# Queueing the modulation's weight blocks earlier in the first part of a hybrid diffusion layer

## The chip, the cores and the metric

One core of a Trainium2 chip runs the whole layer as one program. The metric is device time in microseconds (us) of one execution. TensorE is called PE in the profile, VectorE DVE, ScalarE ACT, GpSimd POOL and SyncE SP; PEld is TensorE's weight load.

## The reference, cut to what matters

The layer takes 512 tokens of width 1024. The change lies in the part before the big input projection, which computes this:

```
x   = x + sincos_2d(512)                              # positions are added
m   = silu(c) @ ada_w + ada_b                         # modulation, 6 x 1024 outputs; the same for c_ctx
h   = sin(fr1 * (z @ w1 + b1)); h = sin(fr2 * (h @ w2 + b2)); h = (h @ w3) * decay    # filter network
kf  = rfft(two-sided kernel made of h)                # spectra of the filters
hx  = rms_norm(x, norm1_g) * (1 + sc1) + sh1          # uses the first 2 x 1024 outputs of m
p   = hx @ w_in                                       # the input projection, everything later needs it
```

Behind it come the context states, the two token mixers (HGRN2 scans and a Hyena long convolution through the spectra `kf`), the merge, the output projection and a mixture of 32 experts (top group, top two experts), whose weights are 190 MB.

## The kernel before, in words

The kernel is one long function. On PE and DVE the instructions run in the order in which they are written (a manual schedule is entered ahead of the filter network). On ACT, POOL and SP a scheduler chooses the order from its own estimates, and each engine then works through its list in that order.

The first part up to the input projection does these things:

- **Loads.** SP issues them: the decay tables `dec` (4 of 256 KB), the tables of the discrete Fourier transform `tabf` (4 of 256 KB), the tokens `x` (4 of 512 KB, list `xts`), the column positions `cpos` (256 KB), and the weight blocks of the modulation `aw` (8 blocks of 1 MB; the first three are one load each into tiles of the pool `w8`, the others two loads of 512 KB each), then `wi`, the first block of `w_in` (two halves of 512 KB, in pieces of 512 B, name `firsts`). (KB and MB are counted in powers of two.) There are eight load semaphores used in turn: a load is issued only once the load eight places before it has landed, so that the start of one load tells when another one was in.
- **The filter network** (`sin_layer`, twice): a small matmul on PE, six operations on DVE, a sine on ACT. Between the two layers' matmuls and the third one, `warm(W3)` puts six matmuls on zeros on PE.
- **The filters** (`filters(0)`, `filters(1)`): matmuls of the third layer into PSUM tiles `ps_t` (four buffers), multiplied by `dec` on DVE into `hp` and `hm`.
- **The positions** (`placed(i)`): for each of four token tiles a one-pass matmul with the row positions `rowp`, added to the left half of `x` on DVE; POOL adds `cpos` to the right half.
- **The modulation** (`ada_row(k)`, k from 0 to 7): for weight block k four matmuls of the 1024 outputs times two columns (`ccs`, the SiLU of c and c_ctx) into the one PSUM tile `pada`. Each is two passes on PE, so that a row is eight entries in the trace.
- **The spectra of the filters** (`dft_steps`, two generators `ks[0]`, `ks[1]`): each takes four pairs of matmuls, and for every two of them one copy on ACT (`dto`) and two operations on DVE (`spec`).
- **The norm** (`normed(i)`): per token tile on ACT a square with a sum (`junk`), a logarithm (`xs`) and an exponential (`xr`), then on DVE the scaled tokens `xn`.
- **Turning and modulating** (`turned`, `ready`, `rest`): the `xn` are transposed on PE; `pada` is copied (`mr`), transposed and made into the scales `gc` and shifts `sc`; `hraw` and the two parts of `hT` follow. `high` and `low` make the two parts `wh` (ACT) and `wl` (POOL for the first, DVE for the second half) of `wi`. With `hT`, `wh` and `wl` the projection starts, three matmuls for each block.

Before the change, the positions of all four tiles stand behind `filters(1)`, then row 0, half of `ks[0]`, row 1, `normed(0)` and `normed(1)`, the rest of `ks[0]`, row 2, `normed(2)` and `normed(3)`, the transpose of the small parameters `prow`, row 3, half of `ks[1]`, rows 4 and 5, twelve transposes of `xn`, rows 6 and 7, and so on.

The lines of the profile: L136 is `mm` (every matmul), L118 `act` (every ACT operation), L332 the filters' product, L337 and L338 the positions, L343 `xn`, L365 to L369 `spec`, L405 the transpose of `prow`, L419 the transposes of `xn`, L429 `mr`, L440 to L442 `sc` and `gc`, L468 `hraw`, L473 the second part of `hT`; L238, L241, L245, L248, L253, L259, L226 and L227 issue the loads of `dec`, `tabf`, `x`, `cpos`, `aw` (first three), `aw` (halves) and the two halves of `wi`; L1622 and L1624 issue the experts' weights.

Of the kernel before, what the change touches and what calls it, by code (L numbers as in the profile page):

```python
# [18 lines left out]
P = 128  # L19
T = 512  # L20
NT = 4
TC = 256
D = 1024
KD = 8
# [8 lines left out]
N8 = 10  # L33
FIX = 4
W1 = 8
W3 = 6
R2 = 3
ORD = (7, 0, 3, 2, 4, 5, 1, 6)
LEAD = 4
# [29 lines left out]
def kernel(ctx: ExitStack, tc: tile.TileContext, a, out, dbg=None):  # L69
    nc = tc.nc  # L70
# [21 lines left out]
    def ps_t(shape=(P, 512)):  # L92
        return pp.tile(list(shape), F32, name="ps_t", tag="t", bufs=4)

    def th(name, shape=(P, 512), dt=F32):

        return fp.tile(list(shape), dt, name=name, tag="h", bufs=NB)
# [9 lines left out]
    def ta(name, shape=(P, 2, 512), dt=F32):  # L107

        return mid.tile(list(shape), dt, name=name, tag="a", bufs=NA)

    def unit(name, shape, dt=F32):

        return base.tile(list(shape), dt, name=name, tag="w8", bufs=NU)
# [11 lines left out]
    def act_set(name):  # L125

        p = nc.scalar.preload_act_table_set(name)
        for r in users:
            tc.add_manual_dep(p.ins, r.ins.name, NOSYNC, reason="activation table")
        users.clear()  # L130
        gate[0] = p
# [3 lines left out]
    def mm(o, l, r, start=True, stop=True):  # L135
        nc.tensor.matmul(o, l, r, start=start, stop=stop)  # L136
# [59 lines left out]
    def warm(n):  # L196

        p = ps_t()
        for i in range(n):
            mm(p, zero[:, 0:P], zero)  # L200
# [22 lines left out]
    def columns2(c0, c1):  # L223

        w = unit("wi", (P, 2, KD, P))
        nc.sync.dma_start(w[:, 0], w_in_v[:, :, c0:c0 + P])  # L226
        nc.sync.dma_start(w[:, 1], w_in_v[:, :, c1:c1 + P])  # L227
        return w[:, 0], w[:, 1]
# [4 lines left out]
        nc.sync.dma_start(w, w_in_v[:, :, c0:c0 + 256])  # L233
        return w[:, :, 0:P], w[:, :, P:2 * P]

    dec = [th(f"dec{m}") for m in range(4)]
    for m in (0, 2, 1, 3):
        nc.sync.dma_start(dec[m], a["k_dec"][m])  # L238
    tabf = [th(f"tabf{m}", (P, 2, 256)) for m in range(4)]
    for m in range(4):  # L240
        nc.sync.dma_start(tabf[m], a["k_tabf"][:, m])  # L241
    xts = []
    for i in range(NT):
        x = ta("x", (P, D))
        nc.sync.dma_start(x, a["x"][0, i * P:(i + 1) * P, :])  # L245
        xts.append(x)
    cpos = th("cpos")
    nc.sync.dma_start(cpos, a["k_cpos"])  # L248
    aws = []
    for k in range(KD):  # L250
        if k < NU:
            w = unit("aw", (P, 2048))
            nc.sync.dma_start(w, ada_v[:, k, 0:2048])  # L253
            aws.append([w[:, j * 512:(j + 1) * 512] for j in range(4)])
        else:
            aws.append([])
            for j in range(2):
                w = ta("aw")
                nc.sync.dma_start(w.rearrange("p a b -> p (a b)"), ada_v[:, k, j * D:(j + 1) * D])  # L259
                aws[k] += [w[:, 0], w[:, 1]]  # L260
        if k == KD - 2:
            firsts = columns2(2560, 3072)

# [2 lines left out]
    def ada_row(k):  # L266
        for j in range(4):
            mm(pada[32 * j:32 * j + 32], ccs[:, k, :], aws[k][j], k == 0, k == KD - 1)
# [19 lines left out]
    def sin_layer(ps, b, f, nm):  # L288
        x = tj(nm + "a", (P, 256))
        V.tensor_scalar(x, ps, pf[:, b:b + 1], pf[:, f:f + 1], op0=OP.add, op1=OP.mult)  # L290
        n = tj(nm + "n", (P, 256))
        V.tensor_scalar(n, x, 1.0 / (2.0 * math.pi), MAGIC, op0=OP.mult, op1=OP.add)
        V.tensor_scalar(n, n, MAGIC, None, op0=OP.subtract)
        V.scalar_tensor_tensor(x, n, -TWO_PI_HI, x, op0=OP.mult, op1=OP.add)
        V.scalar_tensor_tensor(x, n, -TWO_PI_LO, x, op0=OP.mult, op1=OP.add)
        V.tensor_scalar(x, x, 3.1415925, -3.1415925, op0=OP.min, op1=OP.max)
        s = tj(nm + "s", (P, 256))
        act(s, x, AF.Sin)
        return s
# [4 lines left out]
        r = slice(64 * h, 64 * h + 64)  # L304
        mm(pz[r], fw[r, 1], h1[r])
    h2f = sin_layer(pz, 2, 3, "f2")
    warm(W3)
    act_set(EXPLN)


# [10 lines left out]
    def filters(m):  # L321

        ph = []
        for j in range(2):
            for h in range(2):
                r = slice(64 * h, 64 * h + 64)
                ph.append(ps_t())
                mm(ph[-1], h2f[r, m * P:(m + 1) * P], w3[j][r])
        for h in range(2):
            for j, (dst, nm) in enumerate(((hp, "hp"), (hm, "hm"))):  # L330
                dst[m + 2 * h] = tj(f"{nm}{m + 2 * h}")
                V.tensor_mul(dst[m + 2 * h], ph[2 * j + h], dec[m + 2 * h])  # L332

    def placed(i):
        x, p = xts[i], ps_t()
        mm(p, rowp[:, 1, i * P:(i + 1) * P], rowp[:, 0])
        V.tensor_add(x[:, 0:512], x[:, 0:512], p)  # L337
        G.tensor_add(x[:, 512:1024], x[:, 512:1024], cpos)  # L338

    def normed(i):  # L340
        r = rstd_of(xts[i], "x", th("junk", (P, D), BF))
        xn.append(ta("xn", (P, D)))
        V.tensor_scalar(xn[i], xts[i], r, None, op0=OP.mult)  # L343

    def dft_steps(b, srcs_c, srcs_s, new, r, hold=False, tabs=None):

        for cs, src in ((0, srcs_c), (2, srcs_s)):
            p2 = []
            for par in range(2):
                p = ps_mm() if hold and cs and not par else ps_t()  # L350
                for aa in range(2):
                    bs = slice(b * P, (b + 1) * P)
                    if tabs is None:
                        mm(p, tabf[cs + par][:, aa, bs], src[par * 2 + aa], aa == 0, aa == 1)
                    else:
                        mm3(p, tuple(x[:, aa, bs] for x in tabs[cs + par]), src[par * 2 + aa], aa == 0, aa == 1)
                p2.append(p)
                if par == 0:
                    yield
            if hold and cs:  # L360
                yield
            o = th("dto")
            act(o, p2[1], AF.Copy)
            x, y = new()
            V.tensor_add(x, p2[0], o)  # L365
            if cs == 0:
                V.tensor_sub(y, p2[0], o)
            else:
                V.tensor_sub(y, o, p2[0])  # L369
            r += [x, y]  # L370
            yield
# [12 lines left out]
    x, y = hp[0][0:1], hm[0][0:1]  # L384
# [1 line left out]
    V.tensor_scalar(y, x, 0.5, None, op0=OP.mult)  # L386
    V.tensor_scalar(x, x, 0.5, None, op0=OP.mult)
    filters(1)
    for i in range(NT):
        placed(i)  # L390
    ada_row(0)
    kf = [[], []]
    ks = [dft_steps(b, hp, hm, new_a, kf[b], b == 1) for b in range(2)]
    next(ks[0])
    next(ks[0])
    ada_row(1)
    normed(0)
    normed(1)
    next(ks[0])
    next(ks[0])  # L400
    ada_row(2)
    normed(2)
    normed(3)
    pt = ps_t((P, P))
    nc.tensor.transpose(pt, prow, ident)  # L405
    V.tensor_copy(prm, pt)
    ada_row(3)
    next(ks[1])
    next(ks[1])
    ada_row(4)  # L410
    ada_row(5)

    hT = []
# [739 lines left out]
    for n in range(8):  # L1153
        x, e = tj("gb"), tj("gs")
# [111 lines left out]
    for i in range(NT):  # L1266
        x = ta("xacc", (P, D))
# [183 lines left out]
    f = [finish(i) for i in range(NT)]  # L1451
# [680 lines left out]
```

## Time and profile before

| | |
|---|---|
| three runs | 1037.67, 1035.18, 1037.04 us, median 1037.04 |
| profiled execution | 1041.55 us, its span 1039.7 us |
| PE busy | 964.7 us, 93% of the span |
| DVE, ACT, POOL busy | 528.3, 298.3, 184.5 us |
| first 60 us | PE busy 48.43 us, DMA share 0.97, 335 GB/s |
| mean granted clock of PE | 0.961 |

The busy time of an engine is a sum over stages with different limits, and a busy PE is not at its peak, since the ends of matmuls are modelled. The chain of work that ended last says which engine had to be waited for at each moment. A row of the timeline gives start, duration, engine, line, operation, tiles, count, and in brackets how long the engine was idle before it and what ended that.

### The profile page before, as it was taken

The numbers are of one execution on the slowest core, as the hardware profiler recorded it, in microseconds if no ns is written. First come the engines' busy times: TensorE is split into PE (matmuls) and PEld (weight loads), VectorE is DVE, ScalarE is ACT, GpSimd is POOL, SyncE is SP. The second block draws the span as 40 slices with busy tenths as digits, with TensorE's granted clock in tenths as the row PEclk, the third lists the DMA queues.
The fourth block names the chain that finished last, engine by engine and source line by source line (L and its number), as shares of the span: only waits on it lengthen the run. The fifth ranks groups of instructions, "written<-read, shape, count | busy, mean of one in ns | idle before, by whom it ended". The sixth has DMA issues, their size and how long they took to land.

```text
span 1039.7 us, 14041 instructions
## 1 busy us (share of the span) xinstructions
PE 964.7 (93%) x5352; PEld 609.7 (59%) x5352; DVE 528.3 (51%) x886; ACT 298.3 (29%) x492; POOL 184.5 (18%) x212
## 2 busy tenths in 40 slices
PE   6999999999999999999989998999998899978656
PEld 1378888888888887787774463433642245422122
DVE  5565797776775888765375322333232134213024
ACT  1464355475474422243271110000100001000003
POOL 5025244542623310214030000000000000000001
PEclk9999999999999999998999998999998899999877
DMA  9952321121123699346647989999999999999981
GB/s 325 378 157 81 102 61 41 42 82 42 41 77 129 221 278 327 111 155 248 266 184 305 423 346 397 422 421 420 421 381 423 421 420 421 420 420 422 417 297 81
DMA packets 95976, 276.20 MB, mean 266 GB/s; under 512 B 12409, under 2 KB 49365, under 8 KB 72227
## 3 DMA queue, kind: packets, MB, share of 16 engines
q1 hardware_dynamic: 94986, 274.06, 68.6%
q0 software_dynamic: 592, 1.18, 0.4%
q8 instruction: 43, 0.70, 0.3%
q14 instruction: 27, 0.21, 0.1%
q10 hardware_dynamic: 328, 0.04, 0.0%
HBM read 271.05 MB, written 4.21 MB: 265 GB/s over the span
## 4 chain that ended last, share of the span: by engine, by line
issue 45%; PE 41%; DVE 8%; DMA 2%; ACT 2%; POOL 1%; POOLq 0%; SPq 0%; DVEq 0%; ACTq 0%
PE ps_mm L136 31%; PE ps_t L136 8%; DVE wl L147 1%; DMA ew<-in_moe_w_up_dram 1%; DVE yr L632 1%; DMA ada<-in_ada_w_dram 1%; DVE acc L1089 0%; DMA pfr<-in_hy_filt_freq_dram 0%; ACT o L118 0%; DMA cst<-in_k_cst_dram 0%; POOL xacc L2000 0%; PE ps_t L1295 0%; DVE rs L1384 0%; DVE x L517 0%; PE ps_t L929 0%
## 5 line engine op out<-in xcount | busy, mean ns | idle before, releaser
L136 PE MATMUL ps_mm<-hT,wh 128*128 128x512 f32 x768 | 237.6, 391 | 1.3 <-DVE hT L473 0.7
L136 PE MATMUL ps_mm<-ew,xg 128*32 128x512 f32 (+2 forms) x992 | 205.4, 646 | 21.3 <-DMA ew<-in_moe_w_up_dram 15.2
L136 PEld LDWEIGHTS ps_mm<-hT,wh 128*128 128x128 f32 x768 | 144.1, 188 | 31.4 <-DVE hT L473 1.2
L136 PE MATMUL ps_mm<-hT,wl 128*128 128x512 f32 x384 | 155.6, 405 | 1.6 <-DVE wl L147 1.5
L136 PEld LDWEIGHTS ps_mm<-ew,xg 128*32 128x32 f32 (+2 forms) x992 | 63.5, 133 | 149.2 <-issue 106.5
L136 PE MATMUL ps_mm<-ew,hT 128*32 128x512 f32 (+2 forms) x512 | 110.0, 671 | 10.9 <-DMA ew<-in_moe_w_down_dram 10.9
L1713 DVE TENSOR_TENSOR hd<-hd,ps_mm 128x512 f32<-128x512 f32 x13 | 8.9, 688 | 184.2 <-PE ps_mm L136 176.2
L2000 POOL TENSOR_TENSOR xacc<-xacc,fs 128x512 f32<-128x512 f32 x4 | 5.0, 1276 | 481.3 <-ACT o L118 481.3
L136 PEld LDWEIGHTS ps_mm<-hT,wl 128*128 128x128 f32 x384 | 72.2, 188 | 17.0 <-DVE wl L147 2.7
L136 PEld LDWEIGHTS ps_mm<-ew,hT 128*32 128x32 f32 (+2 forms) x512 | 31.7, 137 | 83.2 <-issue 62.8
L147 DVE TENSOR_TENSOR wl<-wi,wh 128x1024 fp32r<-128x1024 f32 x46 | 59.5, 1296 | 23.4 <-ACT wh L118 23.1
L118 ACT ACTIVATE wh<-wi 128x1024 fp32r<-128x1024 f32 x48 | 50.7, 1057 | 48.7 <-PE ps_mm L136 40.1
L1749 DVE TENSOR_TENSOR xacc<-xacc,ps_t 128x512 f32<-128x512 f32 x96 | 58.9, 681 | 0.0
L1726 DVE SCALAR_TENSOR_TENSOR ps_mm<-ps_mm,si,gt 128x512 f32<-128x512 f32 x24 | 18.2, 759 | 78.7 <-PE ps_mm L136 77.4
L118 ACT ACTIVATE yh<-ps_mm 128x512 fp32r<-128x512 f32 x24 | 14.3, 598 | 133.6 <-DVE ps_mm L1726 133.6
L1089 DVE SCALAR_TENSOR_TENSOR acc<-ada,ccs,acc 128x512 f32<-128x512 f32 x56 | 43.0, 832 | 0.0
L136 PE MATMUL ps_t<-yl,ohw 128*128 128x512 f32 x100 | 42.5, 425 | 0.0
L118 ACT ACTIVATE hT<-ps_t 128x512 f32<-128x512 f32 x13 | 7.8, 600 | 118.6 <-PE ps_t L1719 109.2
L136 PE MATMUL ps_mm<-woh,mix 128*128 128x512 f32 x112 | 40.6, 419 | 0.0
L136 PE MATMUL ps_t<-yh,ohw 128*128 128x512 f32 x100 | 39.7, 397 | 0.0
L136 PE MATMUL ps_t<-oh,h2l 128*128 128x512 f32 (+1 forms) x96 | 37.9, 395 | 0.0
L136 PE MATMUL ps_t<-oh,h2h 128*128 128x512 f32 (+1 forms) x96 | 36.1, 376 | 0.0
(450 smaller groups left out, 1550.9 us busy)
## 6 DMA issues: line engine op xcount, KB each, us to landing
ew<-in_moe_w_gate_dram SPq DMA_DIRECT2D x64, 1024.0 KB
ew<-in_moe_w_up_dram SPq DMA_DIRECT2D x62, 1024.0 KB
ew<-in_moe_w_down_dram SPq DMA_DIRECT2D x56, 1024.0 KB
ada<-in_ada_w_dram SPq DMA_DIRECT2D x64, 256.0 KB
wi<-in_w_in_dram SPq DMA_DIRECT2D x24, 512.0 KB
wi<-in_w_in_dram SPq DMA_DIRECT2D x12, 1024.0 KB
ew<-in_moe_w_down_dram SPq DMA_DIRECT2D x16, 512.0 KB
aw<-in_ada_w_dram SPq DMA_DIRECT2D x10, 512.0 KB
```

Of the source, the lines that this page charges most:

```text
L118: r = nc.scalar.activation(o, i, f, **kw)
L136: nc.tensor.matmul(o, l, r, start=start, stop=stop)
L147: V.tensor_sub(lo, view, hi)
L632: V.tensor_sub(yr, yr, t)
L1089: V.scalar_tensor_tensor(acc, w, ccs[:, k, 0:1], acc, op0=OP.mult, op1=OP.add)
L1713: V.tensor_mul(hd, hd, gu[1])
L1726: V.scalar_tensor_tensor(p, p, si[:, 1:2], g, op0=OP.mult, op1=OP.mult)
L1749: V.tensor_add(xs, xs, p)
L2000: G.tensor_mul(xs, xs, fs)
```

## The change

Three moves in the first part:

1. The weight blocks' loads are put in a function `ada_block(k)`. Blocks 0 and 1 are queued first of all, block 2 behind `dec`, block 3 behind `tabf`; the tokens and `cpos` come behind those, then blocks 4 to 7 with `wi` as before.
2. `ada_row(0)` and `ada_row(1)` take the place of the six matmuls on zeros behind the second sine layer.
3. `placed` moves from behind `filters(1)` to behind half of `ks[0]` and row 3; the norms and the spectra behind it are written in another sequence.

```diff
@@ -33,7 +33,6 @@
 N8 = 10
 FIX = 4
 W1 = 8
-W3 = 6
 R2 = 3
 ORD = (7, 0, 3, 2, 4, 5, 1, 6)
 LEAD = 4
@@ -233,21 +232,9 @@
         nc.sync.dma_start(w, w_in_v[:, :, c0:c0 + 256])
         return w[:, :, 0:P], w[:, :, P:2 * P]
 
-    dec = [th(f"dec{m}") for m in range(4)]
-    for m in (0, 2, 1, 3):
-        nc.sync.dma_start(dec[m], a["k_dec"][m])
-    tabf = [th(f"tabf{m}", (P, 2, 256)) for m in range(4)]
-    for m in range(4):
-        nc.sync.dma_start(tabf[m], a["k_tabf"][:, m])
-    xts = []
-    for i in range(NT):
-        x = ta("x", (P, D))
-        nc.sync.dma_start(x, a["x"][0, i * P:(i + 1) * P, :])
-        xts.append(x)
-    cpos = th("cpos")
-    nc.sync.dma_start(cpos, a["k_cpos"])
     aws = []
-    for k in range(KD):
+
+    def ada_block(k):
         if k < NU:
             w = unit("aw", (P, 2048))
             nc.sync.dma_start(w, ada_v[:, k, 0:2048])
@@ -258,6 +245,26 @@
                 w = ta("aw")
                 nc.sync.dma_start(w.rearrange("p a b -> p (a b)"), ada_v[:, k, j * D:(j + 1) * D])
                 aws[k] += [w[:, 0], w[:, 1]]
+
+    dec = [th(f"dec{m}") for m in range(4)]
+    tabf = [th(f"tabf{m}", (P, 2, 256)) for m in range(4)]
+    ada_block(0)
+    ada_block(1)
+    for m in (0, 2, 1, 3):
+        nc.sync.dma_start(dec[m], a["k_dec"][m])
+    ada_block(2)
+    for m in range(4):
+        nc.sync.dma_start(tabf[m], a["k_tabf"][:, m])
+    ada_block(3)
+    xts = []
+    for i in range(NT):
+        x = ta("x", (P, D))
+        nc.sync.dma_start(x, a["x"][0, i * P:(i + 1) * P, :])
+        xts.append(x)
+    cpos = th("cpos")
+    nc.sync.dma_start(cpos, a["k_cpos"])
+    for k in range(4, KD):
+        ada_block(k)
         if k == KD - 2:
             firsts = columns2(2560, 3072)
 
@@ -304,7 +311,8 @@
         r = slice(64 * h, 64 * h + 64)
         mm(pz[r], fw[r, 1], h1[r])
     h2f = sin_layer(pz, 2, 3, "f2")
-    warm(W3)
+    ada_row(0)
+    ada_row(1)
     act_set(EXPLN)
 
 
@@ -386,28 +394,26 @@
     V.tensor_scalar(y, x, 0.5, None, op0=OP.mult)
     V.tensor_scalar(x, x, 0.5, None, op0=OP.mult)
     filters(1)
-    for i in range(NT):
-        placed(i)
-    ada_row(0)
+    ada_row(2)
     kf = [[], []]
     ks = [dft_steps(b, hp, hm, new_a, kf[b], b == 1) for b in range(2)]
     next(ks[0])
     next(ks[0])
-    ada_row(1)
+    ada_row(3)
+    for i in range(NT):
+        placed(i)
+    next(ks[0])
+    next(ks[0])
     normed(0)
     normed(1)
-    next(ks[0])
-    next(ks[0])
-    ada_row(2)
+    ada_row(4)
+    next(ks[1])
+    next(ks[1])
     normed(2)
     normed(3)
     pt = ps_t((P, P))
     nc.tensor.transpose(pt, prow, ident)
     V.tensor_copy(prm, pt)
-    ada_row(3)
-    next(ks[1])
-    next(ks[1])
-    ada_row(4)
     ada_row(5)
 
     hT = []
```

How the instructions stand on three engines, before and after. In these lists a number behind a name tells tiles of one name apart, and a semaphore in brackets is what the instruction waits for (DMAHW are the load semaphores).

The load queue, SP, in the stretch from the last tokens to the first block of `w_in`. Before:

```order
L245 DMA x<-in_x_dram 128x1024
L248 DMA cpos<-in_k_cpos_dram 128x512
L253 DMA aw<-in_ada_w_dram 128x2048 x3
L259 DMA aw<-in_ada_w_dram 128x1024 x8
L226 DMA wi<-in_w_in_dram 128x8x128
L227 DMA wi<-in_w_in_dram 128x8x128
L259 DMA aw<-in_ada_w_dram 128x1024 x2
```

Now:

```order
L246 DMA aw<-in_ada_w_dram 128x1024 x2
L262 DMA x<-in_x_dram 128x1024 x4
L265 DMA cpos<-in_k_cpos_dram 128x512
L246 DMA aw<-in_ada_w_dram 128x1024 x6
L225 DMA wi<-in_w_in_dram 128x8x128
L226 DMA wi<-in_w_in_dram 128x8x128
L246 DMA aw<-in_ada_w_dram 128x1024 x2
```

Before, three of the four token loads stood ahead of `dec`; now four blocks of `aw`, `dec` and `tabf` are ahead of all tokens. The loads ahead of `wi` are the same ones in another sequence.

ACT, from the second copy of `ks[0]` to the one of `ks[1]` (`wh_424` and `wh_426` are the two halves' first parts, `dto_315` the second copy of `ks[0]`, `junk` to `xr` one norm). Before:

```order
L118 ACTIVATE dto_315<-ps_t_312 128x512 [waits PE_49]
L118 ACTIVATE junk_324,xs_325<-x_133 128x1024 [waits DMAHW5_49,DVE_49,Pool_49]
L118 ACTIVATE xs_325<-xs_325,eps_t_88 128x1 [waits Activation_49]
L118 ACTIVATE xr_328<-xs_325 128x1 [waits Activation_49]
L118 ACTIVATE junk_332,xs_333<-x_135 128x1024 [waits DMAHW6_49,DVE_49,Pool_49]
L118 ACTIVATE xs_333<-xs_333,eps_t_88 128x1 [waits Activation_49]
L118 ACTIVATE xr_336<-xs_333 128x1 [waits Activation_49]
L118 ACTIVATE wh_424<-wi_161 128x1024 [waits DMAHW3_49]
L118 ACTIVATE wh_426<-wi_161 128x1024 [waits DMAHW4_49]
L118 ACTIVATE dto_353<-ps_t_350 128x512 [waits PE_49]
```

Now, from the first copy of `ks[0]` (`dto_269`) on, with `dto_300` its second copy:

```order
L117 ACTIVATE dto_269<-ps_t_266 128x512 [waits PE_49]
L117 ACTIVATE wh_417<-wi_161 128x1024 [waits DMAHW3_49]
L117 ACTIVATE wh_419<-wi_161 128x1024 [waits DMAHW4_49]
L117 ACTIVATE dto_300<-ps_t_297 128x512 [waits PE_49]
L117 ACTIVATE junk_305,xs_306<-x_139 128x1024 [waits DMAHW0_49,DVE_49,Pool_49]
L117 ACTIVATE xs_306<-xs_306,eps_t_88 128x1 [waits Activation_49]
L117 ACTIVATE xr_309<-xs_306 128x1 [waits Activation_49]
L117 ACTIVATE junk_313,xs_314<-x_141 128x1024 [waits DMAHW1_49,DVE_49,Pool_49]
L117 ACTIVATE xs_314<-xs_314,eps_t_88 128x1 [waits Activation_49]
L117 ACTIVATE xr_317<-xs_314 128x1 [waits Activation_49]
L117 ACTIVATE dto_331<-ps_t_328 128x512 [waits PE_49]
```

The two conversions of `wi` stood behind all four norms; now they stand ahead of all four norms and of the second copy of `ks[0]`.

PE, around the transpose of `prow` (the one with `cst,prow`; `aw,ccs` is a modulation row, `hp` and `hm` with `tabf` the spectra). Before:

```order
L136 MATMUL ps_mm<-aw,ccs 32x512 x4
L405 MATMUL ps_t<-cst,prow 128x128
L136 MATMUL ps_mm<-aw,ccs 32x512 x4
L136 MATMUL ps_t<-hp_231,tabf_121 128x512
L136 MATMUL ps_t<-hp_250,tabf_121 128x512
L136 MATMUL ps_t<-hp_235,tabf_122 128x512
L136 MATMUL ps_t<-hp_254,tabf_122 128x512
L136 MATMUL ps_mm<-aw,ccs 32x512 x8
L419 MATMUL ps_mm<-cst,xn 128x128 x12
L136 MATMUL ps_mm<-aw,ccs 32x512 x8
```

Now:

```order
L135 MATMUL ps_mm<-aw,ccs 32x512 x4
L135 MATMUL ps_t<-hp_232,tabf_117 128x512
L135 MATMUL ps_t<-hp_251,tabf_117 128x512
L135 MATMUL ps_t<-hp_236,tabf_118 128x512
L135 MATMUL ps_t<-hp_255,tabf_118 128x512
L415 MATMUL ps_t<-cst,prow 128x128
L135 MATMUL ps_mm<-aw,ccs 32x512 x4
L425 MATMUL ps_mm<-cst,xn 128x128 x12
L135 MATMUL ps_mm<-aw,ccs 32x512 x8
```

Between the first half of `ks[1]` and the twelve transposes of `xn` there were two rows; now there are the transpose of `prow` and one row. Rows 6 and 7 stand behind the twelve transposes in both.

## Rows read from the trace of the kernel before

**Rows 1.** Busy time by stage: stretch, length, PE, PEld, DVE, ACT, POOL, clock, DMA, GB/s.
```profile
60.00:480.00 420.00, 417.37 (x2563) 351.47 (x2561) 309.83 (x450) 194.69 (x309) 149.97 (x174) 1.00 0.39 127
```
**Rows 2.** SP's waits from 560 to 620 us: waiter, releaser, total us, times, longest.
```profile
SPq L1624 <- PE ps_mm L136: 30.5, 7, 14.9
SPq L1622 <- PE ps_mm L136: 13.7, 2, 11.1
```
**Rows 3.** The chain that ended last, up to 52 us: start, length, what.
```profile
24.20 0.58 PE ps_t L136
...
26.57 1.86 PE ps_mm L136 x8
...
32.68 1.00 PE ps_mm L136 x8
33.68 3.63 PE ps_t L136 x8
...
45.04 1.46 PE ps_mm L419 x12
46.51 1.85 PE ps_mm L136 x16
...
50.67 0.81 DVE hraw L468
```
**Rows 4.** Timeline of DVE: the last scaled token tile.
```profile
41.23 0.75 DVE L343 TENSOR_SCALAR xn<-x,xr 128x1024 f32<-128x1024 f32 x1 [0.85 <-ACT xr L118]
```
**Rows 5.** Timeline of PE between the sine layers and the filters, 12 to 17 us.
```profile
13.09 2.74 PE L136 MATMUL ps_t<-zero 128*128 128x512 bf16 x6
16.27 0.70 PE L136 MATMUL ps_t<-w3s,f2s 64*128 64x512 f32 x2 [0.44 <-ACT f2s L118]
```
**Rows 6.** PE by short stretches: length, busy (count), granted clock, DMA share, GB/s.
```profile
21.00:22.00 1.00, 0.32 (x1) 1.00 0.96 401
...
23.00:24.00 1.00, 0.00 (x0) 0.50 1.00 418
...
29.50:30.00 0.50, 0.50 (x3) 0.86 1.00 401
...
38.00:39.00 1.00, 1.00 (x13) 1.00 1.09 284
```
**Rows 7.** Timeline of SP's load issues (start, length, line, load).
```profile
10.79 0.33 SPq L241 DMA_DIRECT2D tabf<-in_k_tabf_dram  x1
...
13.43 0.33 SPq L248 DMA_DIRECT2D cpos<-in_k_cpos_dram  x1
...
20.16 0.33 SPq L259 DMA_DIRECT2D aw<-in_ada_w_dram  x1
22.64 0.33 SPq L259 DMA_DIRECT2D aw<-in_ada_w_dram  x1
...
30.20 3.97 SPq L227 DMA_DIRECT2D wi<-in_w_in_dram  x1
```
**Rows 8.** Timeline of POOL: the column positions, four tiles.
```profile
20.28 5.61 POOL L338 TENSOR_TENSOR x<-x,cpos 128x512 f32<-128x512 f32 x4 [10.48 <-DMA cpos<-in_k_cpos_dram]
```
**Rows 9.** Timeline of ACT, 32 to 45 us.
```profile
32.72 0.60 ACT L118 ACTIVATE dto<-ps_t 128x512 f32<-128x512 f32 x1 [15.29 <-PE ps_t L136]
33.21 1.05 ACT L118 ACTIVATE junk<-x 128x1024 bf16<-128x1024 f32 x1
...
34.82 1.04 ACT L118 ACTIVATE junk<-x 128x1024 bf16<-128x1024 f32 x1
...
39.45 1.04 ACT L118 ACTIVATE junk<-x 128x1024 bf16<-128x1024 f32 x1
...
41.05 1.04 ACT L118 ACTIVATE wh<-wi 128x1024 fp32r<-128x1024 f32 x1
42.67 1.06 ACT L118 ACTIVATE wh<-wi 128x1024 fp32r<-128x1024 f32 x1 [0.58 <-DMA wi<-in_w_in_dram]
43.63 0.58 ACT L118 ACTIVATE dto<-ps_t 128x512 f32<-128x512 f32 x1
```

## The prediction

> **What bounds the kernel now.** I first read busy time by stage, to see whether a shift in the first part reaches the end. From 60 to 480 us PE is busy 417.37 of 420 us [rows 1]: the reader is to see that there is no gap in which lost time could be made up. Later the load queue is what runs full, but at the start of the expert stage it is PE that holds it back: between 560 and 620 us SP waits 30.5 + 13.7 us for PE to free weight buffers [rows 2]. So a shift of the first part moves the start of that stream with it, and is worth its full size at the end.
>
> Then the chain of waits for the first part [rows 3]. From 24 to 50 us it runs through PE: spectra, modulation rows, from 45.04 twelve transposes of the scaled tokens (1.46 us), rows 6 and 7 from 46.51 (1.85 us), which end at 46.51 + 1.85 = 48.36; behind them the scales are made and `hraw` starts at 50.67, and from there the projection follows. The norms are not on it: the last `xn` ends at 41.23 + 0.75 = 41.98 [rows 4], 3.1 us before its transposes.
>
> **The change part by part.**
>
> *Rows 0 and 1 for the six matmuls on zeros.* The zeros took 2.74 us from 13.09, and PE then waited for the second sine, until 16.27 [rows 5]. A row takes 1.00 us at full clock and 1.86 us in the stretch where the granted clock was 0.50 [rows 3, 6]. Two rows are 2.0 to 3.7 us from 13.2, so they end between 15.2 and 16.9: a delay of the filters of 0 to 0.7 us. The weights are there: block 0 is the first MB of the queue and block 1 the second. Before, the first MB (two token tiles) was in when the third `tabf` load was issued, 10.79, and the second MB (three token tiles and two of `dec`) when `cpos` was issued, 13.43 [rows 7]. A cost of 0 to 0.7 us, and hidden, as shown below.
>
> *Rows 2 and 3 ahead of the positions.* The modulation still needs rows 6 and 7 behind the transposes, so moving rows earlier shortens only what is ahead of the transposes: there PE no longer has two or three rows of 1.00 us to do. That is a possible gain of up to 3 us, if nothing else holds the transposes.
>
> *Tokens and cpos later.* Ahead of and with `cpos` there are now 8.25 MB in the queue (blocks 0 to 3 are 4, `dec` 1, `tabf` 1, tokens 2, `cpos` 0.25). Before, it was the load with which 4.25 MB were in, by 20.16; a load of 1 MB then took 22.64 - 20.16 = 2.48 us. The 8.25 MB were in at 30.20, when the second half of `wi` could be issued (the load eight places before it had landed) [rows 7]. The queue was full all along (DMA share 0.96 to 1.00 at 21 to 24 us [rows 6]), so `cpos` lands at about 30.2 now, 10 us later. POOL then needs 5.61 us for the four tiles [rows 8]: last token tile ready at 35.8. With ACT free, one norm more (a copy's distance aside, the rhythm is 34.82 - 33.21 = 1.61 us a tile [rows 9], 2.5 us from `junk` to the end of `xn`) gives a last `xn` at 38.3, earlier than 41.98. By this part alone the change would not be slower.
>
> *The order on ACT.* This is the term that decides. The two conversions of `wi` now stand between the first and the second copy of `ks[0]`, ahead of all four norms. They need `wi`, and `wi` has not become earlier: the same 11.25 MB stand ahead of it, and its second half is issued when 8.25 MB are in, 30.20 as before. Before, the second conversion found its half at 42.67, having waited 0.58 us for it [rows 9]. So ACT now stands still from the end of the first copy (about 29 us) until 41 to 42.67, with all norms behind it; where the conversions came after the norms they waited 0.58 us.
>
> From 42.67 on, by the distances of [rows 9]: the second conversion to the next instruction 0.96 us (42.67 to 43.63); two copies `dto` at 0.49 each (32.72 to 33.21); three norms at 1.61, 4.83; the last one from its `junk` to the end of its `xn`, 39.45 to 41.98, 2.53 us [rows 4, 9]. Sum 0.96 + 0.98 + 4.83 + 2.53 = 9.30, so the last `xn` ends at 51.97, 10.0 us later than before.
>
> On PE the transpose of `prow` waits for the second copy of `ks[0]` (ACT frees its buffer), so from about 40 to 44 us nothing runs there; then come `prow`, row 5 and the first three transposes as their `xn` arrive. The fourth one needs the last `xn`. Nine transposes are left: 9 x 1.46 / 12 = 1.10 us, then rows 6 and 7, 1.85 us [rows 3]. At full clock these end at 51.97 + 2.95 = 54.92, against 48.36: **+6.6 us**.
>
> *The clock.* PE had its last matmul at about 21.3 before (0.32 us of work in the slice from 21 to 22); in the slice from 23 to 24 the granted clock was 0.50, the lower of its two levels, and it was full again between 29.5 and 30, some 5.4 us after PE resumed at 24.20 [rows 3, 6]. Now PE has little to do from 40 to 52 us. At the lower level the two rows cost 2 x (1.86 - 1.00) = 1.7 us more and nine transposes up to 1.1 us more: 0 to 2.8 us. I take 2.6, near the upper end, since the gap is longer than the one in the rows, and the 5.4 us to recovery nearly cover the stretch.
>
> **Sum:** 6.6 + 2.6 = **+9.2 us**. The scales, `hraw` and `hT` follow rows 6 and 7 as before. The earlier terms (filters up to 0.7 us late; the second half of `ks[0]`, 3.63 us, at most twice that at the lower clock) are hidden: their results are wanted by ACT only at 43.63, and before, PE had finished both halves of `ks[0]` at 33.68 + 3.63 = 37.3 [rows 3], 6 us earlier. If that cover were gone they would cost 0.7 to 4.3 us. The profiled execution would be 1041.55 + 9.2 = 1050.8; the median of the runs lies 4.5 us below it, so 1037.04 + 9.2 = **1046.2**.
>
> A figure that hangs on one row: where `wi` moves, in pieces of 512 B, the stretch from 38 to 39 us shows 284 GB/s, against 401 to 418 at 21 to 24 us [rows 6]; so its landing is taken at the measured 42.67. The Trainium skill, "DMA: Bandwidth & Descriptors", section "Specifications", states that pieces of 512 B and more go at line rate; by that rule `wi` would be in sooner and the sum would be about 6.6, by the trace it is 9.2.
>
> **The rivals.**
>
> *Sooner or warmer (chance 0.15).* The 4 MB behind `cpos` (blocks 4 to 6 and `wi`) move at the 2.48 us per MB of the other loads: `wi` is in at 30.20 + 4 x 2.48 = 40.1, 2.6 us sooner, and the sum is +6.6. (The page's rule named above would make it so.) Or PE keeps its full clock, also +6.6; both, +4.0. For: the landing was measured once, and each load's issue waited on others. Against: the loads ahead of and behind `wi` are the same ones. Time 1041.0 to 1043.6, likeliest 1043.6.
>
> *Made up later (chance 0.06).* The expert stream, which runs full late, takes part of the shift, because buffers are free sooner relative to its start. For: PE waits there on loads. Against: SP's 44.2 us of waiting for PE [rows 2], which mean the stream started when PE let it, and no gap from 60 to 480 us [rows 1]. Time 0 to +3, likeliest 1038.5.
>
> *Faster (chance 0.03).* ACT's place does not hurt because `wi` is in early: with it by L, the last `xn` is at L + 9.30 and rows 6 and 7 end 2.95 to 5.6 us later, before 48.36 only if L is below 36.1 (33.4 at the lower clock). Then the rows done early pay: the transposes start at about 40 behind row 5, and rows 6 and 7 wait only for block 7, which was in by 46.51 at the latest: a gain of 2 to 4 us, 1034. Against: the 4 MB behind `cpos` would have to land in 36.1 - 30.2 = 5.9 us, where they need 9.9 us at 2.48 us per MB. That the order on ACT is not as listed would come to the same.
>
> *The change does nothing* can be left out: order and loads differ on four engines.
>
> **How the numbers follow.** About 0.3% (3.1 us) can be told from no change. Forecast 0.76 at 1046.2, its own range: the landing of `wi` within 1 us, the clock term from 1.7 to 2.8, and the runs' spread of 1.3: 1043.5 to 1049. The range for 8 in 10 reaches down into the first rival: 1041.5 to 1049. Slower by over 0.3%: 0.76 + 0.15 = 0.91, less 0.01 for its lower edge, 0.90; the second rival is no change, with that edge 0.07; faster 0.03.
>
> **What would show it.** Right: ACT's first conversion of `wi` waits for its load for 10 to 12 us and the second starts near 42.7; the second `dto` at about 43.6; POOL's `cpos` additions from about 30; the last `xn` near 52; PE mostly idle from 40 to 52 us and at 0.50 behind it; rows 6 and 7 ending at 57 to 58; `hraw` at about 60; from there every stage of the same length. Wrong: conversions of `wi` well before 40, or a first `hraw` near 51, or `hraw` late and the end of the span not.

## The result, and the profile after

| | before | after |
|---|---|---|
| median of four runs (us) | 1037.36 (1035.18 to 1038.17) | 1045.65 (1045.13 to 1047.64) |
| ratio, 95% interval | | 1.0087 [1.0066, 1.0107] |
| profiled execution, span (us) | 1041.55, 1039.7 | 1045.33, 1043.4 |
| first `hraw` (us) | 50.67 | 59.97 |

The change makes the kernel slower by 8.3 us by the medians; the interval of the ratio is +6.8 to +11.1 us. The forecast was 1046.2. The profiled execution of before was 4 us above its median and the one after stands at its median, so the two spans may not be subtracted (that would give 3.7). What can be compared is where each stage begins: the first `hraw`, from which the projection follows, is 9.3 us later.

Busy time by stage of the changed kernel (stretch, length, PE, PEld, DVE, ACT, POOL, clock, DMA, GB/s):

```profile
0.00:60.00 60.00, 41.77 (x156) 14.72 (x157) 24.91 (x60) 13.75 (x28) 15.43 (x23) 0.86 0.91 320
60.00:480.00 420.00, 416.11 (x2552) 348.84 (x2550) 311.33 (x456) 198.94 (x314) 144.00 (x170) 1.00 0.38 120
```

PE lost 6.7 us of work in the first 60 us (48.43 before) and ran them at a mean clock of 0.86 (0.94 before). From 60 to 480 us it is full as before [rows 1]: nothing is made up there. SP's longest waits for PE early in the expert stage are there again (560 to 630 us, 10 us more than in [rows 2], since the stage begins later; waiter, releaser, total us, times, longest):

```profile
SPq L1630 <- PE ps_mm L135: 30.5, 7, 14.9
SPq L1628 <- PE ps_mm L135: 16.3, 3, 11.1
```

They are 30.5 and 16.3 us, before 30.5 and 13.7 [rows 2]: the weight stream still starts when PE lets it.

The chain that ended last, 20 to 61 us (start, length, what):

```profile
20.92 9.00 DMA cpos<-in_k_cpos_dram
29.94 12.61 DMA wi<-in_w_in_dram
...
43.54 0.58 ACT dto L117
...
51.10 0.77 DVE xn L351
51.91 2.18 PE ps_mm L425 x9
54.09 3.57 PE ps_mm L135 x16
57.66 1.11 PE ps_t L425 x8
...
59.97 0.82 DVE hraw L474
```

Before, this stretch ran through PE [rows 3]. Now it is the load of `wi`, then ACT with the norms, the last `xn`, nine transposes, rows 6 and 7. ACT's timeline shows the place where time was lost (start, duration, and in brackets the idle time before and what ended it):

```profile
26.60 0.60 ACT L117 ACTIVATE dto<-ps_t 128x512 f32<-128x512 f32 x1 [9.02 <-PE ps_t L135]
40.93 1.06 ACT L117 ACTIVATE wh<-wi 128x1024 fp32r<-128x1024 f32 x1 [13.74 <-DMA wi<-in_w_in_dram]
42.58 1.06 ACT L117 ACTIVATE wh<-wi 128x1024 fp32r<-128x1024 f32 x1 [0.59 <-DMA wi<-in_w_in_dram]
43.54 0.58 ACT L117 ACTIVATE dto<-ps_t 128x512 f32<-128x512 f32 x1
44.02 1.05 ACT L117 ACTIVATE junk<-x 128x1024 bf16<-128x1024 f32 x1
...
49.31 1.04 ACT L117 ACTIVATE junk<-x 128x1024 bf16<-128x1024 f32 x1
```

For 13.74 us ACT waits for `wi`, and for the last 5.9 of them all tokens are ready: POOL finished adding `cpos` at 30.06 + 4.95 = 35.0. The second conversion starts at 42.58, before 42.67 [rows 9]; `wi` has not moved, the norms have moved behind it. PE in short stretches (length, busy and count, granted clock, DMA share, GB/s):

```profile
38.00:40.00 2.00, 0.00 (x0) 1.00 1.16 292
40.00:42.00 2.00, 0.00 (x0) 0.69 1.07 363
...
54.00:56.00 2.00, 2.00 (x13) 0.50 0.87 239
56.00:58.00 2.00, 2.00 (x11) 0.54 0.14 22
58.00:60.00 2.00, 2.00 (x15) 1.00 0.00 0
```

PE's last matmul before the gap ends at 37.5. Between 40 and 42 us its clock falls to the lower of the two levels, and rows 6 and 7 are over before it is back.

### The profile page after: what moved, and what is told of

Read it like the earlier page. It is cut to its first block, busy times and chain, and to the rows that moved or that the text cites. A ratio compares the mean times of both kernels' runs of the same rounds, so it can differ in the third digit from the quotient of the medians.

```text
span 1043.4 us, 14033 instructions
## 1 busy us (share of the span) xinstructions
PE 957.1 (92%) x5346; PEld 609.0 (58%) x5346; DVE 524.0 (50%) x886; ACT 298.3 (29%) x492; POOL 183.8 (18%) x212
## 4 chain that ended last, share of the span: by engine, by line
issue 45%; PE 39%; DVE 7%; DMA 5%; ACT 3%; POOL 1%; SPq 0%; POOLq 0%; ACTq 0%; DVEq 0%
PE ps_mm L135 30%; PE ps_t L135 7%; DMA wi<-in_w_in_dram 1%; DVE wl L146 1%; DMA ew<-in_moe_w_up_dram 1%; DMA cpos<-in_k_cpos_dram 1%; DMA tabf<-in_k_tabf_dram 1%; DMA aw<-in_ada_w_dram 1%; DVE yr L638 1%; DMA ada<-in_ada_w_dram 1%; ACT junk L117 0%; DVE acc L1095 0%; DMA cT<-in_c_dram 0%; ACT o L117 0%; POOL xacc L2006 0%
## 5 line engine op out<-in xcount | busy, mean ns | idle before, releaser
L135 PE MATMUL ps_mm<-ew,xg 128*32 128x512 f32 (+2 forms) x992 | 198.8, 615 | 24.5 <-DMA ew<-in_moe_w_up_dram 17.5
```

## The experiments

The theory: ACT works through its list in order, the list has the conversions of `wi` ahead of the norms, and the loss is that place (6.6 us) and the lower clock behind the gap (2.6 us). The rivals to be excluded: that the later tokens or the rows' new places cost the time themselves, that `wi` or its small pieces are the cause, that the clock had no part. The lines of each kernel are shifted by its edit; the tiles' names are the same. The kernel before ran beside each group of experiments with a median of its own (1037.56 us beside the first four, 1039.20 beside the next four, 1039.45 beside the last), so kernels are compared by their ratios to it and not by their medians.

### The norms ahead of the conversions, all else as in the changed kernel

```diff
-        act(ws[j][0], firsts[j], AF.Copy)
+        r = act(ws[j][0], firsts[j], AF.Copy)
+        tc.add_manual_dep(r.ins, last_xr[0].ins.name, NOSYNC, reason="norms first")
```

> The changed kernel with one edit: the two conversions of wi on ACT are made to follow the last norm. Theory (ACT's order is the whole loss): POOL's additions from 30 us set the norms, last xn at about 38 instead of 51.9; transposes at about 40; rows 6 and 7 wait only for weight block 7, which is queued behind wi and should be in at about 45; rows 6 and 7 end at about 46 instead of 57.7, hraw near 48.5. Total 1034 to 1036, some 10 us below the changed kernel and 1 to 3 below the kernel before. Rival (the later tokens, or the rows moved ahead, cost the time themselves): it stays at 1043 to 1046.

Measured: 1035.56 us (12 runs), 0.9989 [0.9975, 1.0003] of before; first `hraw` at 49.65. In the built program two instructions stand elsewhere, the two conversions on ACT; nothing else on any engine has changed its place. That takes back the whole loss, 10.3 us at `hraw`. ACT's timeline:

```profile
32.58 0.60 ACT L117 ACTIVATE dto<-ps_t 128x512 f32<-128x512 f32 x1 [5.71 <-PE ps_t L135]
33.08 1.05 ACT L117 ACTIVATE junk<-x 128x1024 bf16<-128x1024 f32 x1
...
39.47 1.04 ACT L117 ACTIVATE junk<-x 128x1024 bf16<-128x1024 f32 x1
41.07 1.04 ACT L117 ACTIVATE wh<-wi 128x1024 fp32r<-128x1024 f32 x1
42.50 1.06 ACT L117 ACTIVATE wh<-wi 128x1024 fp32r<-128x1024 f32 x1 [0.39 <-DMA wi<-in_w_in_dram]
```

The norms begin at 33.08, behind the second copy, for which ACT waits 5.71 us for PE. So the last `xn` is out at about 42, as before the change: with ACT's list mended, the tokens' new place in the queue neither wins nor costs. That is not the 38.3 which the prediction gave for a free ACT. The total fell into the expected range although these steps did not come out: rows 6 and 7, from 43.20, took 4.24 us, in part waiting for block 7, and `hraw` was expected at 48.5.

### The kernel before, with the conversions put ahead of the norms

```diff
     ada_row(1)
+    ws = [[...] for w in firsts]
+    for j in range(2):
+        convs.append(act(ws[j][0], firsts[j], AF.Copy))
     normed(0)
...
-        act(junk, x, AF.Square, accum_out=ss)
+        r = act(junk, x, AF.Square, accum_out=ss)
+        if convs:
+            tc.add_manual_dep(r.ins, convs[-1].ins.name, NOSYNC, reason="conversions first")
```

> The kernel before with one edit: the two conversions of wi on ACT are made to precede the first norm; loads, rows and positions as before. Theory: ACT stands still until wi is in at 42.7, the last xn is near 52, the transpose of prow waits for the second copy of ks[0] at about 47 and one half of ks[1] and three rows follow it, so that the transposes start between 54 and 58 instead of 45: total 9 to 13 us above the kernel before, 1046 to 1050. Rival (the loads' and rows' new places are the cause): within 2 us of the kernel before.

Measured: 1045.41 us (4 runs), 1.0086 [1.0053, 1.0118]; `hraw` at 59.29. SP, POOL and PE have the order of before, and DVE too, but for two `spec` that follow a copy on ACT; the loss is that of the change (1.0087). ACT:

```profile
42.88 1.06 ACT L118 ACTIVATE wh<-wi 128x1024 fp32r<-128x1024 f32 x1 [2.34 <-DMA wi<-in_w_in_dram]
43.85 1.04 ACT L118 ACTIVATE junk<-x 128x1024 bf16<-128x1024 f32 x1
```

The first norm stands at 43.85, before at 33.21 [rows 9]. So the place on ACT is enough for the loss without any other part of the change, and by the experiment above the rest of the change costs nothing without it. The loss, 8.9 us by the ratio, is just below the 9 to 13 expected, and one step was another: the transpose of `prow` did not wait (40.14); PE waited 3.73 us for a copy in the middle of the first half of `ks[1]`, until 47.12.

### PE kept at work in the gap

```diff
+    def fill(n):
+        for i in range(n):
+            mm(pre[2], zero[:, 0:P], zero)
+
+    fill(24)
     pt = ps_t((P, P))
...
     ada_row(5)
+    fill(4)
...
+        if i < 3:
+            fill((6, 8, 6)[i])
```

> The changed kernel with 48 matmuls on zeros put into PE's idle time between the first half of ks[1] and the last xn, written into a buffer that the transposes fill later; nothing else. Theory (a part of the loss is the lower clock behind the idle time): nine transposes take 1.1 instead of 2.18 us and rows 6 and 7 take 1.85 instead of 3.57, so that hraw starts at about 57.2 instead of 60.0: total 2.8 us below the changed kernel, about 1042.9. Rival (the clock costs nothing, or the filling delays the transposes as much as it saves): within 1 us of 1045.7.

Measured: 1043.44 us (6 runs), 1.0069 [1.0045, 1.0092]; `hraw` at 57.52, 2.5 us sooner than in the changed kernel. PE by stretch, and its rows 6 and 7:

```profile
54.00:56.00 2.00, 2.00 (x19) 1.00 0.88 226
```

```profile
53.34 1.92 PE L135 MATMUL ps_mm<-aw,ccs 128*32 128x512 f32 x16
```

The rows take 1.92 us instead of the 3.64 of the changed kernel's timeline, on the same operands, at a granted clock of 1.00 instead of 0.50. At `hraw` the clock's part of the loss is 2.5 us. By the ratios (1.0087 and 1.0069) it is 1.9, with intervals that overlap, so in the total it is not shown by itself.

### `wi` queued behind all weight blocks, norms ahead

```diff
     for k in range(4, KD):
         ada_block(k)
-        if k == KD - 2:
-            firsts = columns2(2560, 3072)
+    firsts = columns2(2560, 3072)
```

> The first experiment's kernel with one more edit: wi is queued behind weight block 7 instead of ahead of it. Theory: block 7 is in at about 40, rows 6 and 7 end at about 42, hraw near 44.5, wi is still in at 42.6, and its parts are made by 45, before the projection needs them: total 6 us below the kernel before, about 1031. Rival (with hraw that early wi's conversions become the wait, or the later stages take it back): 1034 to 1036, as the first experiment.

Measured: 1036.91 us (10 runs), 1.0000 [0.9985, 1.0016]; `hraw` at 50.25. The 6 us that the theory expected did not come, nor `hraw` at 44.5. `wi` comes 2.7 us later than in the first experiment (second conversion at 45.17 instead of 42.50), and the time doesn't follow it: behind the norms, ACT has that slack. The last `xn` still comes at 42, for the same reason as there, and PE, waiting for it, is at 0.50 again:

```profile
42.25 2.18 PE L426 MATMUL ps_mm<-cst,xn 128*128 128x128 f32 x9 [1.27 <-DVE xn L352]
44.36 3.63 PE L135 MATMUL ps_mm<-aw,ccs 128*32 128x512 f32 x16
```

### Norms where the tokens become ready, `wi` last

```diff
     next(ks[0])
-    next(ks[0])
     normed(0)
     normed(1)
+    next(ks[0])
     ada_row(4)
     next(ks[1])
-    next(ks[1])
     normed(2)
     normed(3)
+    next(ks[1])
```

The copies `dto` are held behind the last `xr` until the norms are done, the conversions behind the last of these `dto`, and the operations on `lbm` behind the scales.

> The changed kernel with three edits: ACT takes each pair of norms ahead of the spectra's copies, so that a norm waits for its tokens alone; the conversions of wi follow the norms and the copies; wi is queued behind weight block 7 (and the small bounds' operations on DVE come behind the scales). Theory: in the first and the fourth experiment the norms still began at 33, behind the second copy of ks[0], though the first tokens are whole at 31.3, and the last xn came at 41 to 42; now it comes at about 39, PE has no gap long enough for its clock to fall, rows 6 and 7 end at about 42, hraw starts at 44 to 45; wi is in at 45.2, its parts by 48. Total 4 to 6 us below the kernel before, 1031.5 to 1033.5. Rival (wi's landing at 45.2 is now the end: its parts are awaited by the projection as long as the norms were): 1035 to 1037.

Measured: 1034.91 us (12 runs), 0.9959 [0.9942, 0.9977], faster than both kernels; `hraw` at 46.75, 3.9 us sooner than before. ACT's first norm now waits for the tokens, and PE's transposes for the last `xn`:

```profile
31.43 1.06 ACT L117 ACTIVATE junk<-x 128x1024 bf16<-128x1024 f32 x1 [4.54 <-POOL x L348]
```

```profile
39.33 1.21 PE L430 MATMUL ps_mm<-cst,xn 128*128 128x128 f32 x9 [0.46 <-DVE xn L353]
40.46 2.14 PE L135 MATMUL ps_mm<-aw,ccs 128*32 128x512 f32 x16
```

The kernel above has the same loads, with the norms behind the copies, and gained nothing; so it is the norms' place that lets the loads pay. How much of the gain is owed to the early weight blocks is argued and not shown, since no run made the same edits on the kernel before. There PE had next to no idle time up to the end of rows 6 and 7 that earlier norms could have shortened (stretch, length, PE, PEld, DVE, ACT, POOL, clock, DMA, GB/s, before):

```profile
24.20:48.36 24.16, 24.11 (x106) 7.96 (x106) 14.30 (x25) 10.04 (x22) 4.07 (x3) 0.89 1.04 393
```

Two microseconds went at the last scale; see the last experiment.

### The same, with `wi` ahead of block 7 as in the change

> As the fifth experiment, but with wi queued ahead of weight block 7 as in the changed kernel. Theory (in the first experiment rows 6 and 7 took 4.24 us because block 7 came late, at about 46): rows 6 and 7 still end at about 47, hraw starts at about 49, total as the first experiment, 1035 to 1036. Rival (the norms' end at 41 to 42 was the limit of the first experiment): hraw at 45 to 46, 1031 to 1033.

The edit is the one above without the move of `wi`. Measured: 1037.29 us (11 runs), 0.9982 [0.9964, 1.0000]; `hraw` at 52.3. Here the transposes are done at 40.7, and row 7 waits for its block:

```profile
44.11 1.06 PE L135 MATMUL ps_mm<-aw,ccs 128*32 128x512 f32 x4 [2.40 <-DMA aw<-in_ada_w_dram]
46.86 1.92 PE L135 MATMUL ps_mm<-aw,ccs 128*32 128x512 f32 x4 [1.69 <-DMA aw<-in_ada_w_dram]
```

With the norms early, the last block of the modulation decides, and `wi` ahead of it in the queue takes its time. `hraw`, expected at 49, is 1.6 us later than before while the total is 1.9 us lower; that doesn't fit the other kernels. The profiled executions show where this one makes it up. At 465.71 a copy on DVE (`mk`) still stands 2.07 us later than before (463.64); at 504.03 another operation (`ss`) is 1.37 us ahead of before (505.40). Between them lies a stretch in which PE's granted clock was 0.86 before and 1.00 here (columns as above, before and then this kernel):

```profile
475.00:500.00 25.00, 22.86 (x101) 18.77 (x100) 11.89 (x20) 7.39 (x16) 5.85 (x4) 0.86 0.47 181
```

```profile
475.00:500.00 25.00, 23.12 (x120) 19.10 (x118) 14.64 (x21) 7.53 (x16) 7.64 (x5) 1.00 0.63 237
```

The 0.14 of 25 us, 3.5 us at full clock, is about what this kernel gains there (2.07 + 1.37 = 3.44). In the other kernels the clock of this stretch does not follow `hraw` (0.86 with the norms at the tokens and `wi` last, 0.93 in the changed kernel), and one execution of each kernel was profiled. Whether the other executions of this one keep their clock there too is not shown.

### `wi` in pieces of 1 KB

```diff
-            firsts = columns2(2560, 3072)
+            firsts = columns(2560)
```

One load of 256 neighbouring columns takes the place of two loads of 128 columns, in the same place of the queue.

> The changed kernel, with the first block of w_in loaded as 256 neighbouring columns in one load of 1 MB, in pieces of 1 KB, instead of two loads of 128 columns in pieces of 512 B; the second half of the block is thus other columns than the reference's, in time the same work. If pieces of 512 B move more slowly (284 GB/s in the trace): wi is in earlier than 42.6, at 40 to 41, ACT's second conversion and hraw come 1.5 to 2.5 us earlier than in the changed kernel (42.6 and 60.0). If they move at the same rate, as the Trainium skill's page "DMA: Bandwidth & Descriptors" states of pieces from 512 B on: within 0.5 us of 42.6 and 60.0.

Measured: a single run, 1046.23 us, no interval; `hraw` at 60.2. ACT, then the rates from 38 to 40 us (stretch, length, POOL's busy time, clock, DMA share, GB/s) and the packets of the same stretch, of this kernel and of the changed one:

```profile
42.36 2.00 ACT L117 ACTIVATE wh<-wi 128x1024 fp32r<-128x1024 f32 x2 [15.33 <-DMA wi<-in_w_in_dram]
```

```profile
38.00:40.00 2.00, 0.00 (x0) 1.00 1.11 358
DMA packets 642, 0.72 MB, mean 358 GB/s; under 512 B 15, under 2 KB 618, under 8 KB 642
```

```profile
38.00:40.00 2.00, 0.00 (x0) 1.00 1.16 292
DMA packets 1137, 0.58 MB, mean 292 GB/s; under 512 B 16, under 2 KB 1134, under 8 KB 1137
```

For comparison, the packets from 36 to 38 us of the kernel with the norms ahead and `wi` behind all weight blocks:

```profile
DMA packets 229, 0.82 MB, mean 410 GB/s; under 512 B 29, under 2 KB 29, under 8 KB 229
```

Nearly all packets in the first two are the pieces of `wi` (603 of 642 and 1118 of 1137), and those of 1 KB move faster, 358 against 292 GB/s. The gain is small: counted from POOL's first addition of `cpos` (30.61 here, 30.06 in the changed kernel), all of `wi` is in after 11.75 us instead of 12.52; three other kernels with the same queue and pieces of 512 B need 12.25 to 12.50. It does not reach `hraw`, because with a single load the first conversion, too, waits for all of `wi`, until 42.36 instead of 40.93, and the second copy comes at 44.27 instead of 43.54. The numbers are those of the expectation's second branch, but not for its reason. In this form the size of the pieces is no way out of the wait.

### `wi` queued ahead of the tokens

```diff
     ada_block(3)
+    firsts = columns2(2560, 3072)
     xts = []
...
-        if k == KD - 2:
-            firsts = columns2(2560, 3072)
```

> The changed kernel with wi queued ahead of the tokens (behind weight block 3); on ACT the conversions then stand ahead of even the first copy of ks[0]. Theory (the stall is the wait for wi, whatever the place in ACT's list): wi is in at about 26 to 28, the conversions wait for nothing that matters, cpos comes at about 35, the tokens are whole at 40, the last xn at about 43, block 7 is in by about 45; rows 6 and 7 end at 46 to 47, hraw at about 49. Total 1035 to 1037, like the kernel before and 9 below the changed kernel. Rival (the place on ACT costs by itself, or tokens 5 us later cost as much): 1041 or more.

Measured: 1041.9 us (10 runs), 1.0029 [1.0011, 1.0047]; `hraw` at 53.1. Most of the loss goes, not all of it: the scheduler now has the conversions ahead of the first copy too.

```profile
27.07 1.06 ACT L117 ACTIVATE wh<-wi 128x1024 fp32r<-128x1024 f32 x1 [9.41 <-DMA wi<-in_w_in_dram]
28.85 1.06 ACT L117 ACTIVATE wh<-wi 128x1024 fp32r<-128x1024 f32 x1 [0.72 <-DMA wi<-in_w_in_dram]
29.81 0.58 ACT L117 ACTIVATE dto<-ps_t 128x512 f32<-128x512 f32 x1
37.89 0.60 ACT L117 ACTIVATE dto<-ps_t 128x512 f32<-128x512 f32 x1 [7.49 <-PE ps_t L135]
```

PE waits 2.74 us for that copy to free a PSUM buffer, and the second copy comes only at 37.89, the norms behind it. The orders on PE and DVE are those of the changed kernel. The chain that ended last runs from the landing of `wi` (28.83) through a conversion, the first copy and PE's spectra to the norms; the tokens, ready at 34.76 + 4.95 = 39.71, are not on it. So the same mistake in an earlier place costs 3 us by the ratio. That lies between the two ranges expected, and `hraw` was expected at 49.

### The first low part on DVE instead of POOL

```diff
     high(0)
-    low(0, G)
     ready(0)
+    low(0, V)
     high(1)
```

Made on the kernel with the norms at the tokens and `wi` last.

> The kernel with the norms at the tokens and wi last, but the first low part of the weights (wl) is made by DVE behind the first hraw, and no longer by POOL beside the scales. Theory: the last scale (gc, 128x8) took 2.09 us because it ran while POOL made wl for 2.35 us; with POOL idle there it takes 0.17, and the first hraw starts 1.9 us sooner, at about 44.8 instead of 46.7. Rival: the 2 us belong to the operation itself, which waits for something else at that place (the second use of gc); then it takes 2.09 again and hraw stays at 46.7 or later. Total: by the theory 0 to 1.9 us below 1034.9, since wl now stands on DVE for 1.8 us between the first and the second hraw; by the rival 0 to 2 us above it.

Measured: 1033.94 us (6 runs), 0.9952 [0.9934, 0.9970]; not to be told apart from 0.9959 [0.9942, 0.9977] without the edit. The operation in dispute, without the edit and with it:

```profile
44.38 0.17 DVE L455 SCALAR_TENSOR_TENSOR gc<-gc,prm 128x8 f32<-128x8 f32 x1
44.45 2.35 POOL L470 TENSOR_TENSOR wl<-wi,wh 128x1024 fp32r<-128x1024 f32 x1 [8.90 <-ACT wh L117]
...
44.74 2.09 DVE L455 SCALAR_TENSOR_TENSOR gc<-gc,prm 128x8 f32<-128x8 f32 x1
```

```profile
45.34 0.17 DVE L455 SCALAR_TENSOR_TENSOR gc<-gc,prm 128x8 f32<-128x8 f32 x1
45.43 0.81 DVE L483 TENSOR_SCALAR hraw<-ps_mm,gc,sc 128x512 f32<-128x512 f32 x1
```

With POOL idle it takes 0.17 us. From the first scale's start to the first `hraw` it is 45.43 - 44.71 = 0.72 us instead of 46.75 - 44.10 = 2.65: the price of the neighbour was 1.9 us, as the theory said. `hraw` came only 1.3 us sooner, because in this execution `mr` and the scales began 0.6 us later; and the first matmul of the projection starts at 49.46, without the edit at 49.28, since `wl` and then the second `hraw` stand on DVE ahead of the `hT` part. The gain at the scales is given back there.

### How `hraw` and the time go together

| kernel | `hraw`, us against 50.67 | total, us by the ratio (of 1037), with its interval |
|---|---|---|
| the change | +9.3 | +9.0 [+6.8, +11.1] |
| before, conversions early | +8.6 | +8.9 [+5.5, +12.2] |
| PE kept at work | +6.9 | +7.2 [+4.7, +9.5] |
| `wi` ahead of the tokens | +2.4 | +3.0 [+1.1, +4.9] |
| norms first | -1.0 | -1.1 [-2.6, +0.3] |
| norms first, `wi` last | -0.4 | 0.0 [-1.6, +1.7] |
| norms at the tokens, `wi` last | -3.9 | -4.3 [-6.0, -2.4] |
| the same, low part on DVE | -5.2 | -5.0 [-6.8, -3.1] |
| norms at the tokens | +1.6 | -1.9 [-3.7, 0.0] |

In eight of nine kernels the end follows the first `hraw` within the interval. The last is the exception named above. The profiled executions show how far the shift at `hraw` is handed on unchanged: the copy `mk` stands 9.29 us later in the changed kernel than before,

```profile
463.64 0.17 DVE L1211 COPY mk<-ps_t 128x24 f32<-128x24 f32 x1
```

```profile
472.93 0.17 DVE L1217 COPY mk<-ps_t 128x24 f32<-128x24 f32 x1
```

and in the other kernels of the table its shift is that of `hraw` within 0.5 us, except with the low part on DVE, where it is 3.5 us and not 5.2 (460.10).

## Why the prediction was right, point by point

- **What bounds the kernel.** That a shift of the first part is worth its full size at the end held [rows 1, 2]; the table shows it for gains and losses, and up to 464 us the traces do. "Made up later" did not happen.
- **Rows 0 and 1** took 3.64 us from 13.24, the top of the 2.0 to 3.7 given, and the filters' matmuls began at 16.81 instead of 16.27 [rows 5]: 0.54 us, hidden as said.
- **Rows 2 and 3 ahead**, a gain of up to 3 us "if nothing else holds the transposes": in the changed kernel the last `xn` held them. Where the norms followed the tokens and block 7 stood ahead of `wi`, `hraw` came 3.9 us sooner than before; with block 7 behind `wi`, row 7 waited for it.
- **Tokens and `cpos`** landed for POOL at 30.06, forecast 30.2. POOL took 4.95 us and not 5.61 [rows 8].
- **The order on ACT** was the term that decides. The steps came out one by one: second conversion 42.58 (42.67), second copy 43.54 (43.63), last `xn` ended at 51.85 (51.97). The first two experiments show it as the cause from both sides.
- **The clock.** Nine transposes took 2.18 us and the rows 3.64, rows 6 and 7 over at 57.66 by the chain (forecast 54.92 + 2.6 = 57.5). With PE kept at work `hraw` came 2.5 us sooner, forecast 2.6.
- **Smaller misses.** ACT waited 13.74 us, not 10 to 12: the first copy was done at 27.2 and not at 29. PE had no gap from 20 to 24 us and its clock did not fall there (1.00, before 0.50 from 23 to 24 [rows 6]), and DVE's operation on one row of `hm` took 0.41 us instead of 1.37, with POOL no longer adding `cpos` beside it. That wait ends with `wi` in any case, so nothing followed.
- **"With ACT free, the last `xn` at 38.3"** was wrong, and was no term of the sum. The norms also stand behind the copies, which wait for PE; with ACT free the last `xn` came at 42. It came at 39.3 where the norms were written ahead of the copies.
- **The rival "Faster"** took the last `xn` at L + 9.30 for `wi` in at L. With the second conversion at 28.85 that is 38.2; its transposes were at 47.83. Its formula left out that the copies behind the conversions hold PE up.
- **The rival "Sooner or warmer"** did not come about, but its price held: with PE kept at work the loss is 7.2 us by the ratio, forecast 6.6. On `wi` sooner: the stretch from 38 to 40 us shows 292 GB/s, where before had 284 [rows 6], and its packets are pieces of 512 B; with pieces of 1 KB it shows 358. From 36 to 38 us of the kernel with the norms ahead and `wi` last, with pieces larger than 2 KB, it is 410. The Trainium skill, "DMA: Bandwidth & Descriptors", section "Specifications", has pieces from 512 B up at line rate; these rates don't agree with it.

What stays open is why the norms at the tokens with `wi` ahead of block 7 end 1.9 us below before with an `hraw` 1.6 us later (the clock from 475 to 500 us is a candidate, seen in one execution), and what earlier norms would do in the kernel before.

## What to carry to other kernels

When loads are moved in a queue, read what an automatic scheduler then does to the engines whose order nobody wrote: here two conversions that wait for a load went ahead of work that was ready, and cost 0.9%. An instruction that waits for a late load belongs in the list of an in-order engine behind everything that the load does not hold up; an explicit edge on each did that. The kernel with the earlier blocks became faster than before, by 0.4%, only when the consumers followed the new order (norms where the tokens are ready, the last weight block ahead of `wi`).

## What the runs showed of the hardware

A small operation on DVE can be held up by a large one on POOL. The scale of 128 x 8 elements took 0.17 us alone and 2.09 us when it started inside POOL's `wl`: it ended at 44.74 + 2.09 = 46.83, POOL at 44.45 + 2.35 = 46.80. The operations between them on the same engine (`sc`, `gc` from PSUM, at 44.47 and 44.54) took their usual 0.16 us beside the same POOL instruction. Not all of DVE's operations are held up, then; this one has two inputs in SBUF, those one in PSUM and one in SBUF. The kernel before has another case: `lbm`, also with two inputs in SBUF, ended at 42.22 + 2.34 = 44.56 and POOL's `wl` at 42.17 + 2.37 = 44.54; in the changed kernel, with POOL idle, `lbm` took 0.17 us. The Trainium skill, "SBUF — State Buffer", section "SBUF: two separate sides", says that the two engines share a pair of ports as an exclusive lock, which a DVE operation with two SBUF inputs needs, and that the loser waits until the other's instruction is over; the trace agrees, to 0.03 us.

The clock fell late and came back late in the changed kernel: without a matmul from 37.5 us on, it was still 1.00 from 38 to 40 us and 0.50 from 42 us on; with PE busy without a break from 52 us, the stretch from 56 to 58 still shows 0.54. The work behind this wait was paid at the lower level: some three microseconds of it, by the run with PE kept at work, cost 2.5 more at `hraw`.
